# A two-layer MLP's second product: some operands built earlier, and the last ones in another order and on another engine

## The chip, the cores and the metric

The kernel runs on one NeuronCore of a Trainium2 chip. TensorE (PE) multiplies, VectorE (DVE), ScalarE (ACT) and GpSimd (POOL) do the elementwise work, and SyncE (SP) issues most DMAs. The metric is the device time of one execution in microseconds; a result is the median of the runs made.

## The reference, cut to what matters

The reference is a transformer block on 1024 tokens of width 1024: two attention branches, gates, an output projection, a squared-ReLU MLP and a last RMSNorm. The change touches its end alone:

```python
h2 = rms_norm(x, norm_mlp_g[l], NORM_EPS)
x = x + jnp.square(jax.nn.relu(h2 @ w_ff1[l])) @ w_ff2[l]      # 1024 -> 4096 -> 1024
return rms_norm(x, norm_final_g, NORM_EPS)
```

## The kernel before, in words

Everything is float32, but a matmul takes its operands in a shorter format. So each operand is split into two halves: `hi`, a copy by ScalarE in that format (line 1273), and `lo`, what is left, `x - hi`, by VectorE or GpSimd (line 1274). A product is then three matmuls: hi by hi, hi by lo and lo by hi (lines 1358 to 1360). `operand(x, to, eng)` makes the two halves, with `eng` for the lower one.

The second MLP product sums over 4096 hidden units, which are worked through in pairs of 128-blocks: 16 pairs of 256. The hidden activations `f` lie in DRAM, written by the first product (`squared`, line 1147), and are read back as raw blocks `ra`; the weights come as raw blocks `rb`. There are five groups: pairs 0 and 1 (the first group), pairs 2 to 5, 6 to 9 and 10 to 13, and at the end pairs 14 and 15.

A group is a 2 by 2 block product: the output is split into two halves of the tokens and two halves of the columns, the sum into two halves as well. Each of the first four groups uses seven block products instead of eight, in the order of `PRODUCTS`: 1, 5, 6, 3, 7, 2, 4. Product 1 multiplies raw blocks. Products 5, 6 and 3 take running sums: `fs5` of the activations (line 1302) and `ws5` of the weights (line 1310), which are overwritten from one product to the next. `a5` and `b5` are the halves of product 5's operands, and so on. In the first group a product is 24 matmuls, in the next three groups it is 48. Sums that two outputs share wait in `sum5` and `sum6`; the PSUM results are added into the residual (`xb` and `acc`, lines 1371 and 1373).

The last group, pairs 14 and 15, is done without the seven products: for each block of 128 tokens the four halves `alast` and `blast` are multiplied, column half 0 first, then column half 1 (`last_product`), and the final norm follows for that token block.

Where a raw block lies is fixed by a table of tiles (`HOME`) which the last pair of the first MLP product still reads, so its loads start as that product lets go of one tile after another. The halves of products 3, 6 and 4 of the first group lie partly in tiles (`own`) whose room was that of the first MLP product's results `c`: they can be written when the last `f` block has been written to DRAM. The residual `xb` is loaded into the same room, with the same wait.

The program's text does not set the order on an engine alone: a scheduler merges the instructions of neighbouring parts into one queue for each engine, and an engine takes its queue strictly in order. So an instruction that waits holds up all that stand behind it.

Of the kernel before, what the change touches and what calls it, by code (L numbers as in the profile page):

```python
# [77 lines left out]
def f(ap):  # L78

    return ap.bitcast(F32)  # L80
# [3 lines left out]
def tile_hybrid_block(ctx: ExitStack, tc: tile.TileContext, t: dict, out: bass.AP):  # L84
    nc = tc.nc
# [847 lines left out]
    for n in range(len(steps) + LAG):  # L933
        if n < len(steps):
            h, qb = steps[n]
# [10 lines left out]
        if 0 < n <= len(steps):  # L946
            h, qb = steps[n - 1]
            b_combine(heads[h], qb)
        later()
        if n >= LAG:  # L950
            h, qb = steps[n - LAG]
# [40 lines left out]
    for u in range(8 * AH + LAGA):  # L992
        h, n = u // 8, u % 8
# [108 lines left out]
    for n in range(16):  # L1102
# [9 lines left out]
        for j in range(4):  # L1112
            i = 4 * half + j
# [46 lines left out]
    def ff1_operands(n, ra, rb):  # L1160
        if n == NEARLY - 1:
            s1 = p5.tile([P, DK, P], F32, tag="u", name=f"s1_{n}", bufs=2)
        else:
            s1 = pf.tile([P, DK, P], F32, tag="s1", name=f"s1_{n}", bufs=2)
        return rest_operands(f"f{n}", ra, rb, s1)
# [18 lines left out]
    n = NEARLY - 1  # L1184
    operands = []
# [15 lines left out]
    for i, n in enumerate(order):  # L1201
        if i:
# [3 lines left out]
            operands = ff1_operands(n, *cur)  # L1206
# [11 lines left out]
    def place(nm, z, name, dt=F32):  # L1218
        pool = phb if nm in ("B11", "B21") else pht
        return pool.tile([P, GROUP, 512], dt, tag=f"h{nm}{z}", name=name)  # L1220
# [35 lines left out]
    def own(tag, name):  # L1256
        return p5.tile([P, GROUP, 512], F32R, tag=tag, name=name)

    def operand_set(name):

        sets[0] ^= 1
        if sets[0]:
            return {side: [place(nm, z, f"{side}{name}_{z}", F32R) for z in range(2)] for side, nm in (("a", "B11"), ("b", "B21"))}
        return {"a": [place("T3", 1, f"a{name}_0", F32R), own("a1", f"a{name}_1")],
                "b": [own("b0", f"b{name}_0"), own("b1", f"b{name}_1")]}

    def couple(to, c):
        return {side: [z[:, 2 * c:2 * c + 2, :] for z in to[side]] for side in "ab"}

    def operand(x, to, eng):  # L1270

        hi, lo = to
        nc.scalar.activation(hi, x, AF.Copy)  # L1273
        eng.tensor_tensor(lo, x, f(hi), op=ALU.subtract)  # L1274
        return hi, lo


    PRODUCTS = ((1, 0), (5, 0), (6, 1), (3, 1), (7, 0), (2, 0), (4, 1))

    def ff2_group(pairs, r, count):  # L1280
        begin = pairs[0] == 0
        couples = range(len(pairs) // 2)
        temp = {}

        def block(kind, i, j, c):
            return r.get((kind, i, j, c))

        def fresh(side, name, c):
            temp[side, c] = wp.tile([P, 2, 512], F32, tag="wh" if side == "a" else "wl", name=name, bufs=3)
            return temp[side, c]  # L1290

        def prepare(which, c, to):
            name = f"{which}_{pairs[2 * c]}"
            a = {1: (0, 0), 2: (0, 1), 4: (1, 1)}.get(which)
            b = {1: (0, 0), 2: (1, 0), 3: (1, 1)}.get(which)
            if a:
                s = block("a", *a, c)
            else:
                s = fresh("a", f"fs{name}", c) if which in (5, 7) else temp["a", c]
                x, y, op = {5: (block("a", 1, 0, c), block("a", 1, 1, c), ALU.add), 6: (s, block("a", 0, 0, c), ALU.subtract),  # L1300
                            3: (block("a", 0, 1, c), s, ALU.subtract), 7: (block("a", 0, 0, c), block("a", 1, 0, c), ALU.subtract)}[which]
                nc.vector.tensor_tensor(s, x, y, op=op)  # L1302
            if b:
                u = block("b", *b, c)
            else:

                u = temp["b", c] if which in (6, 4) else block("b", 1, 1, c) if which == 7 else fresh("b", f"ws{name}", c)
                x, y = {5: (block("b", 0, 1, c), block("b", 0, 0, c)), 6: (block("b", 1, 1, c), u),
                        4: (block("b", 1, 0, c), u), 7: (block("b", 1, 1, c), block("b", 0, 1, c))}[which]
                nc.vector.tensor_tensor(u, x, y, op=ALU.subtract)  # L1310
            return operand(s, to["a"], nc.vector), operand(
                u, to["b"], nc.vector if which == 1 or begin and which == 5 else nc.gpsimd)

        def target(which):
            if which in (5, 6):
                if begin:
                    sums[which] = place("T4", which - 5, f"sum{which}")
                return sums[which]
            half, col = {1: (0, 0), 2: (0, 0), 3: (0, 1), 4: (1, 0), 7: (1, 1)}[which]
            return res[half][:, :, 512 * col:512 * col + 512]  # L1320

        def begin_places(k, which):

            if k % 4 == 0 and k < 5:
                late["set"] = {side: [place(nm, z, f"{side}{which}_0_{z}", F32R) for z in range(2)]
                               for side, nm in (("a", "B11"), ("b", "B21"))}
            if k in (0, 1, 4, 5):
                return couple(late["set"], k % 4)
            if k == 2:
                x, y = place("T3", 1, "a6_0", F32R), place("T3", 0, "b6_0", F32R)  # L1330
            elif k == 3:
                x, y = own("a1", "a3_0"), own("b0", "b3_0")
            else:
                x, y = own("b1", "a4_0"), place("T3", 1, "b4_0", F32R)
            return {"a": [x[:, 0:2, :], x[:, 2:4, :]], "b": [y[:, 0:2, :], y[:, 2:4, :]]}

        banks = [None, None]
        for k, (which, more) in enumerate(PRODUCTS):
            if begin:
                ops = [prepare(which, 0, begin_places(k, which))]  # L1340
            else:
                to = operand_set(f"{which}_{pairs[0]}")
                ops = [prepare(which, c, couple(to, c)) for c in couples]
            if not more:
                if (k + count) % 2:
                    banks[k % 2] = [bank([P, 512], tag, f"p{which}_{pairs[0]}_{j}") for j, tag in enumerate(("T", "T", "mm", "gm"))]
                else:
                    banks[k % 2] = [bank2(f"p{which}_{pairs[0]}_{j}") for j in range(2)]
            here = banks[k % 2]
            target_of = target(which)  # L1350
            for j in range(4):
                wide = len(here) == 2
                acc = here[j // 2][:, 512 * (j % 2):512 * (j % 2) + 512] if wide else here[j]
                c = slice(j * P, j * P + P)
                for i in range(len(pairs)):
                    (ah, al), (bh, bl) = ops[i // 2]
                    last = i == len(pairs) - 1
                    nc.tensor.matmul(acc, ah[:, i % 2, c], bh[:, i % 2, :], start=i == 0 and not more, stop=False, skip_group_check=bool(more))  # L1358
                    nc.tensor.matmul(acc, ah[:, i % 2, c], bl[:, i % 2, :], start=False, stop=False, skip_group_check=bool(more))  # L1359
                    nc.tensor.matmul(acc, al[:, i % 2, c], bh[:, i % 2, :], start=False, stop=last, skip_group_check=bool(more))  # L1360
                if wide and j % 2 == 0:
                    continue
                into = target_of[:, j - 1:j + 1, :] if wide else target_of[:, j, :]
                of = here[j // 2].rearrange("p (j n) -> p j n", j=2) if wide else acc
                if begin and which in (5, 6):
                    nc.scalar.activation(into, of, AF.Copy)
                elif begin and which == 1:

                    x = wp.tile([P, 2, 512], F32, tag="wh", name=f"p1_0_{j}", bufs=3)
                    nc.scalar.activation(x, of, AF.Copy)  # L1370
                    nc.vector.tensor_tensor(into, x, into, op=ALU.add)
                else:
                    nc.vector.tensor_tensor(into, of, into, op=ALU.add)
            if begin and which == 6:
                load_b(pairs, r, 1, 0)
# [22 lines left out]

    r = pair_raws((NP2 - 2, NP2 - 1))
    blocks_a, blocks_b = {}, {}  # L1400
    for i in range(2):
        to = operand_set(f"last{i}")
        for j in range(2):
            blocks_a[i, j] = operand(r["a", i, j, 0], couple(to, j)["a"], nc.vector)
        for h in range(2):
            blocks_b[h, i] = operand(r["b", h, i, 0], couple(to, h)["b"], nc.gpsimd)
    for x in (res[0][:, :, 512:1024], res[1][:, :, 0:512], sums[5]):
        nc.vector.tensor_tensor(x, x, sums[6], op=ALU.add)
    nc.vector.tensor_tensor(res[1][:, :, 512:1024], res[1][:, :, 512:1024], sums[5], op=ALU.add)
# [17 lines left out]
    i = NT - 1  # L1427
    ss = p5.tile([P, 2], F32, tag="n_ss2", name="n3_last_ss")
    sq = wp.tile([P, D], F32, tag="wr", name="n3_last_sq", bufs=2)
    for h in range(2):  # L1430
# [3 lines left out]
        a = acc1[i][:, cols]  # L1434
# [35 lines left out]
```

## Time and profile before

| | us |
|---|---|
| median of 3 runs | 1673.32 |
| lowest, highest run | 1667.09, 1675.45 |
| profiled execution | 1674.86 |
| its span | 1673.1 |
| TensorE busy in the span | 1557.9 (93%) |
| VectorE busy | 1181.4 (71%) |
| ScalarE busy | 697.6 (42%) |
| GpSimd busy | 585.3 (35%) |

The second MLP product takes the stretch from 1333 us to the end. TensorE is busy nearly throughout. The share of VectorE, 71% over the span, is far higher there: 48.10 of the 50 us from 1350 to 1400, 49.86 of those from 1550 to 1600. An engine's mean share says little here; what counts is where TensorE stands still, and what it waits for.

### The profile page before, as it was taken

The page shows a single profiled execution, that of the slowest core. Times are in us where ns is not written, and L with a number is a line of the kernel's source. Part 1 is how long each engine was busy: PE and PEld are TensorE (multiplying, and loading weights), DVE is VectorE, ACT ScalarE, POOL GpSimd, SP SyncE. Part 2 cuts the span into 40 slices and gives each one's busy share as a digit, 9 for nine tenths or more (in the row PEclk, how much of TensorE's full clock was granted, in tenths as well). Part 3 has the DMA queues.
Part 4 walks back from the last instruction along what each step waited for, and adds up shares of the span by engine and source line. Part 5 has one row for each costly group of instructions (what it writes and reads, how often), then busy time and mean ns, then how long its engine had stood idle before and what let it go on. Part 6 is the DMA issues. An engine that isn't in the chain of part 4 may idle for free. (4 is left out here: it accounts for less than half of the span.)

```text
span 1673.1 us, 20932 instructions
## 1 busy us (share of the span) xinstructions
PE 1557.9 (93%) x7832; PEld 1299.2 (78%) x7832; DVE 1181.4 (71%) x1367; ACT 697.6 (42%) x1064; POOL 585.3 (35%) x289
## 2 busy tenths in 40 slices
PE   8899889988789998989999999899999989999998
PEld 6798667766577887988887878687888867888776
DVE  5976798698688996645547357644355599898984
ACT  4432122232467774544433236444444552333331
POOL 1534444555232332012220003533333344354551
PEclk8999899998999999999999999999999999999999
DMA  6367566555767557656557333444333571423112
GB/s 214 125 210 215 164 196 223 175 184 163 263 194 233 200 191 271 204 180 215 156 162 278 110 130 94 120 128 130 114 101 101 179 268 51 163 74 116 51 38 101
DMA packets 214389, 271.23 MB, mean 162 GB/s; under 512 B 12784, under 2 KB 136848, under 8 KB 214288
## 3 DMA queue, kind: packets, MB, share of 16 engines
q1 hardware_dynamic: 200464, 236.33, 44.4%
q10 hardware_dynamic: 13824, 33.56, 5.3%
q8 instruction: 62, 1.02, 0.3%
q14 instruction: 39, 0.32, 0.1%
HBM read 183.81 MB, written 80.27 MB: 158 GB/s over the span
## 5 line engine op out<-in xcount | busy, mean ns | idle before, releaser
L1359 PE MATMUL p<-b,a 128*128 128x512 f32 x392 | 154.7, 395 | 5.1 <-DVE b L1274 5.1
L1358 PE MATMUL p<-b,a 128*128 128x512 f32 x392 | 154.2, 393 | 3.0 <-ACT a L1273 3.0
L1360 PE MATMUL p<-b,a 128*128 128x512 f32 x392 | 154.4, 396 | 2.0 <-DVE a L1274 1.9
L1274 POOL TENSOR_TENSOR b<-ws,b 128x1024 fp32r<-128x1024 f32 x20 | 61.4, 3088 | 95.3 <-ACT b L1273 85.3
L1359 PEld LDWEIGHTS p<-b,a 128*128 128x128 f32 x392 | 74.2, 189 | 23.0 <-DVE b L1274 6.0
L1274 POOL TENSOR_TENSOR b<-rb,b 128x1024 fp32r<-128x1024 f32 x21 | 70.8, 3390 | 54.7 <-ACT b L1273 46.7
L1360 PEld LDWEIGHTS p<-b,a 128*128 128x128 f32 x392 | 74.0, 189 | 20.1 <-DVE a L1274 3.9
L1358 PEld LDWEIGHTS p<-b,a 128*128 128x128 f32 x392 | 74.1, 189 | 19.8 <-ACT a L1273 3.4
L689 PE MATMUL sb<-kb,qb 128*128 128x512 f32 x256 | 74.7, 416 | 15.1 <-ACT p L694 8.8
L694 ACT ACTIVATE p<-sb,mn 128x1024 f32<-128x1024 f32 x64 | 71.3, 1116 | 38.5 <-DVE mn L692 23.7
L692 DVE TENSOR_REDUCE mn<-sb 128x1 f32<-128x1024 f32 x64 | 76.8, 1217 | 9.7 <-PE sb L689 9.2
L265 DVE TENSOR_TENSOR s<-w 128x512 f32<-128x512 f32 x15 | 16.2, 1081 | 85.8 <-DMA w<-in_w_ff 85.8
L156 POOL TENSOR_SCALAR n_y<-n_ss 128x1 f32<-128x1 f32 x23 | 5.1, 222 | 187.7 <-ACT n_xn L163 183.2
L803 PE MATMUL sa<-kh_a,zq 128*128 128x256 f32 x256 | 68.9, 300 | 1.2 <-DVE mna L812 1.2
L828 DVE TENSOR_TENSOR pta<-ta,pta 128x512 fp32r<-128x512 f32 x64 | 43.8, 688 | 33.9 <-ACT pta L827 33.7
L689 PEld LDWEIGHTS sb<-kb,qb 128*128 128x128 f32 x256 | 45.9, 192 | 27.9 <-ACT p L694 13.1
L1273 ACT ACTIVATE a<-fs 128x1024 fp32r<-128x1024 f32 x28 | 29.4, 1054 | 90.6 <-PE p L1359 71.3
L803 PE MATMUL sa<-kl_a,zq 128*128 128x256 f32 x256 | 65.8, 288 | 0.0
L246 POOL TENSOR_TENSOR wt_f_l<-w,wt_f_h 128x1024 fp32r<-128x1024 f32 x15 | 36.1, 2404 | 83.0 <-ACT wt_f_h L245 70.2
L816 ACT ACTIVATE sm<-sm,mna 128x512 f32<-128x512 f32 x64 | 46.1, 720 | 32.4 <-DVE mna L812 31.8
L827 ACT ACTIVATE pta<-ta 128x512 fp32r<-128x512 f32 x64 | 37.6, 591 | 52.2 <-PE ta L823 44.5
L1145 ACT ACTIVATE c<-c 128x512 f32<-128x512 f32 x64 | 39.9, 624 | 46.6 <-DVE c L292 34.9
(442 smaller groups left out, 4966.4 us busy)
## 6 DMA issues: line engine op xcount, KB each, us to landing
w<-in_w_in SPq DMA_DIRECT2D x32, 512.0 KB, 4.3
qk<-r ACTq DMA_DIRECT2D x32, 512.0 KB, 4.8
f<-c ACTq DMA_DIRECT2D x64, 256.0 KB, 2.0
rb<-in_w_ff SPq DMA_DIRECT2D x32, 512.0 KB, 4.6
ra<-f SPq DMA_DIRECT2D x64, 256.0 KB, 5.0
w<-in_w_ff SPq DMA_DIRECT2D x30, 512.0 KB, 4.2
vb<-vb SPq DMA_DIRECT2D x16, 512.0 KB, 6.6
rot<-raw SPq DMA_DIRECT2D x64, 128.0 KB, 4.5
```

Source lines behind the costliest of these rows:

```text
L689: nc.tensor.matmul(sps[:, 512 * n:512 * n + 512], q[:, z, (qb % 4) * P:(qb % 4 + 1) * P], o.k[m][:, 512 * n:512 * n + 512], start=z == 0, ...
L692: nc.vector.tensor_reduce(mn, sps, axis=AX.X, op=ALU.min)
L694: nc.scalar.activation(p, sps, AF.Exp, scale=-1.0, bias=mn, accum_out=o.zz[qb][:, m:m + 1])
L803: nc.tensor.matmul(ps[:, 0:CM], zq[:, n % 4, c, :], kk[:, c * CM:(c + 1) * CM], start=c == 0 and kk is o.kh, stop=c == NCLS - 1 and kk is ...
L816: nc.scalar.activation(sm, sm, AF.Exp, scale=-1.0, bias=mn, accum_out=stat[h % 2][:, n:n + 1])
L827: nc.scalar.activation(view[0], tv, AF.Copy)
L828: nc.vector.tensor_tensor(view[1], tv, f(view[0]), op=ALU.subtract)
L1145: nc.scalar.activation(c, c, AF.Relu)
L1274: eng.tensor_tensor(lo, x, f(hi), op=ALU.subtract)
L1358: nc.tensor.matmul(acc, ah[:, i % 2, c], bh[:, i % 2, :], start=i == 0 and not more, stop=False, skip_group_check=bool(more))
L1359: nc.tensor.matmul(acc, ah[:, i % 2, c], bl[:, i % 2, :], start=False, stop=False, skip_group_check=bool(more))
L1360: nc.tensor.matmul(acc, al[:, i % 2, c], bh[:, i % 2, :], start=False, stop=last, skip_group_check=bool(more))
```

## The change

Two places. In the first group, `prepare` was called for each product just ahead of its matmuls; now, at product 1, the operands of products 1 and 5 are both prepared ahead of product 1's matmuls, and the others at their products as before. In the last group, the halves were written in the order of the first index of two loops: the activations of token half 0, the weights of column half 0, then those of half 1, with every lower half of a weight on GpSimd. Now the weights of column half 0 come first, then the activations of token half 0, the weights of column half 1, the activations of token half 1; and the lower halves of the two weight blocks of column half 1 are VectorE's. What is computed, and where it is stored, is the same.

```diff
@@ -1335,9 +1335,13 @@
         banks = [None, None]
+        ready = {}
         for k, (which, more) in enumerate(PRODUCTS):
             if begin:
-                ops = [prepare(which, 0, begin_places(k, which))]
+
+                for n in (0, 1) if k == 0 else (k,) if k > 1 else ():
+                    ready[n] = [prepare(PRODUCTS[n][0], 0, begin_places(n, PRODUCTS[n][0]))]
+                ops = ready.pop(k)
             else:
@@ -1398,12 +1402,13 @@
     r = pair_raws((NP2 - 2, NP2 - 1))
     blocks_a, blocks_b = {}, {}
-    for i in range(2):
-        to = operand_set(f"last{i}")
+    to = [couple(operands, z) for operands in (operand_set("last0"), operand_set("last1")) for z in range(2)]
+    for side, i in (("b", 0), ("a", 0), ("b", 1), ("a", 1)):
         for j in range(2):
-            blocks_a[i, j] = operand(r["a", i, j, 0], couple(to, j)["a"], nc.vector)
-        for h in range(2):
-            blocks_b[h, i] = operand(r["b", h, i, 0], couple(to, h)["b"], nc.gpsimd)
+            if side == "a":
+                blocks_a[i, j] = operand(r["a", i, j, 0], to[2 * i + j]["a"], nc.vector)
+            else:
+                blocks_b[j, i] = operand(r["b", j, i, 0], to[2 * i + j]["b"], nc.vector if i else nc.gpsimd)
```

What the scheduler makes of it shows in the engines' queues. In the rows below a name's middle number is the first pair of its group, the last number a serial one.

VectorE at the passage from the first MLP product (`c..._15`) to product 1 and product 5 of the first group, before:

```order
L1274 TENSOR_TENSOR a1_0_1_11477<-ra00_0_11450,a1_0_0_11476 128x1024
L292 TENSOR_TENSOR c12_15_11367<-zf15_11371,c12_15_11367 128x512
L294 TENSOR_TENSOR c21_15_11368<-zf15_11371,u_15_11366 128x512
L1310 TENSOR_TENSOR ws5_0_11518<-rb11_0_11461,ws5_0_11518 128x1024
L295 TENSOR_TENSOR c22_15_11369<-zf15_11371,c21_15_11368 128x512
L298 TENSOR_TENSOR c21_15_11368<-4f15_11372,c21_15_11368 128x512
L1302 TENSOR_TENSOR fs5_0_11516<-ra10_0_11455,ra11_0_11458 128x1024
L1274 TENSOR_TENSOR a1_0_1_11477<-fs5_0_11516,a1_0_0_11476 128x1024
```

And now:

```order
L1274 TENSOR_TENSOR a1_0_1_11477<-ra00_0_11450,a1_0_0_11476 128x1024
L1302 TENSOR_TENSOR fs5_0_11484<-ra10_0_11455,ra11_0_11458 128x1024
L292 TENSOR_TENSOR c12_15_11367<-zf15_11371,c12_15_11367 128x512
L294 TENSOR_TENSOR c21_15_11368<-zf15_11371,u_15_11366 128x512
L1274 TENSOR_TENSOR a1_0_1_11477<-fs5_0_11484,a1_0_0_11476 128x1024
L295 TENSOR_TENSOR c22_15_11369<-zf15_11371,c21_15_11368 128x512
L1302 TENSOR_TENSOR fs5_0_11484<-fs5_0_11484,ra00_0_11450 128x1024
L298 TENSOR_TENSOR c21_15_11368<-4f15_11372,c21_15_11368 128x512
L1310 TENSOR_TENSOR ws5_0_11486<-rb11_0_11461,ws5_0_11486 128x1024
```

The activation operand of product 5 (`fs5` and the lower half made of it, which shares a tile with product 1's and so is printed as `a1`) moved ahead of the last four additions of the first MLP product, and the next sum `fs5` of product 6 moved ahead of the weight sum.

ScalarE from the last copies of the first MLP product on, before (`sum5` and `p1` are copies out of PSUM):

```order
L1147 DMA f15_9039<-c21_15_11368 128x512
L1370 ACTIVATE p1_0_1_11498<-p1_0_0_11484 128x1024
L1370 ACTIVATE p1_0_3_11513<-p1_0_1_11485 128x1024
L1273 ACTIVATE b3_0_11595<-rb11_0_11461 128x1024
L1273 ACTIVATE a1_0_0_11476<-fs5_0_11516 128x1024
L1273 ACTIVATE a4_0_11704<-ra11_0_11458 128x1024
L1366 ACTIVATE sum5_11528<-p5_0_0_11524 128x512
L1366 ACTIVATE sum5_11528<-p5_0_1_11525 128x512
L1273 ACTIVATE a6_0_11557<-fs5_0_11516 128x1024
```

And now:

```order
L1374 ACTIVATE p1_0_1_11506<-p1_0_0_11492 128x1024
L1146 ACTIVATE c21_15_11368<-c21_15_11368 128x512
L1374 ACTIVATE p1_0_3_11521<-p1_0_1_11493 128x1024
L1147 DMA f15_9039<-c21_15_11368 128x512
L1370 ACTIVATE sum5_11528<-p5_0_0_11524 128x512
L1370 ACTIVATE sum5_11528<-p5_0_1_11525 128x512
L1273 ACTIVATE b6_0_11558<-ws5_0_11486 128x1024
L1370 ACTIVATE sum5_11528<-p5_0_2_11526 128x512
L1273 ACTIVATE a3_0_11594<-fs5_0_11484 128x1024
L1370 ACTIVATE sum5_11528<-p5_0_3_11527 128x512
L1273 ACTIVATE b3_0_11595<-rb11_0_11461 128x1024
```

The upper half of product 5 is out of this piece (it stands earlier); that of `b6`, which stood ahead of the first row shown of before, now stands behind two copies of product 5's results, and `a3`, which product 3's lower half on VectorE waits for, behind three.

VectorE at the last group, the difference (`sum6` is the last shared sum, `ff_last0` the first token block's result):

```order
-L1408 TENSOR_TENSOR acc1_8065<-acc1_8065,sum6_11565 128x4x512
-L1274 TENSOR_TENSOR alast1_1_13297<-ra10_14_13271,alast1_0_13296 128x1024
-L1274 TENSOR_TENSOR alast1_1_13297<-ra11_14_13274,alast1_0_13296 128x1024
-L1423 TENSOR_TENSOR xb_11471<-ff_last0_13312,xb_11471 128x1024
...
+L1413 TENSOR_TENSOR acc1_8065<-acc1_8065,sum6_11565 128x4x512
+L1274 TENSOR_TENSOR blast1_1_13291<-rb01_14_13269,blast1_0_13290 128x1024
+L1274 TENSOR_TENSOR blast1_1_13291<-rb11_14_13277,blast1_0_13290 128x1024
+L1274 TENSOR_TENSOR alast1_1_13289<-ra10_14_13271,alast1_0_13288 128x1024
+L1274 TENSOR_TENSOR alast1_1_13289<-ra11_14_13274,alast1_0_13288 128x1024
+L1428 TENSOR_TENSOR xb_11471<-ff_last0_13312,xb_11471 128x1024
```

The two lower halves of the weights of column half 1 stand on VectorE ahead of those of the activations of token half 1; GpSimd's queue has lost two instructions there. TensorE's queue now begins the second token block while it waits for the first of them.

## Rows read from the trace of the kernel before

**Rows 1.** Waits of TensorE, 1300 to 1420 us: total us, times, longest

```profile
PE p L1359 <- DVE b L1274: 5.1, 2, 5.0
PE p L1358 <- ACT a L1273: 3.0, 1, 3.0
PE p L1360 <- DVE a L1274: 1.3, 2, 0.9
```

**Rows 2.** Waits of TensorE, 1590 us to the end

```profile
PE ff_last L1416 <- POOL blast L1274: 3.0, 2, 1.6
```

**Rows 3.** Timeline, TensorE: start us, us, what, [idle before <- releaser]

```profile
1333.18 0.39 PE L1358 MATMUL p<-b,a 128*128 128x512 f32 x1
...
1338.42 0.39 PE L1360 MATMUL p<-b,a 128*128 128x512 f32 x1
1341.81 0.50 PE L1358 MATMUL p<-b,a 128*128 128x512 f32 x1 [3.00 <-ACT a L1273]
...
1360.45 0.40 PE L1359 MATMUL p<-b,a 128*128 128x512 f32 x1
...
1376.74 0.39 PE L1358 MATMUL p<-b,a 128*128 128x512 f32 x1
...
1383.90 0.79 PE L1359 MATMUL p<-b,a 128*128 128x512 f32 x1 [4.96 <-DVE b L1274]
```

**Rows 4.** Stretch of product 1, second group: length; busy us (instructions) by engine; clock, DMA

```profile
1376.74:1395.20 18.46, 13.35 (x49) 10.21 (x48) 16.67 (x14) 2.01 (x2) 5.78 (x2) 0.82 0.19 58
```

**Rows 5.** Timeline, VectorE, first group

```profile
1335.20 3.40 DVE L1302 TENSOR_TENSOR fs<-ra,ra 128x1024 f32<-128x1024 f32 x1
1341.79 2.56 DVE L1274 TENSOR_TENSOR a<-fs,a 128x1024 fp32r<-128x1024 f32 x1 [3.19 <-ACT a L1273]
1344.28 1.21 DVE L1310 TENSOR_TENSOR rb<-rb,rb 128x1024 f32<-128x1024 f32 x1
...
1371.36 0.68 DVE L1373 TENSOR_TENSOR xb<-p,xb 128x512 f32<-128x512 f32 x1
...
1380.49 3.35 DVE L1274 TENSOR_TENSOR b<-rb,b 128x1024 fp32r<-128x1024 f32 x1
```

**Rows 6.** Timeline, GpSimd, first group

```profile
1335.12 2.40 POOL L1274 TENSOR_TENSOR b<-ws,b 128x1024 fp32r<-128x1024 f32 x1 [11.99 <-ACT b L1273]
...
1351.23 9.03 POOL L1274 TENSOR_TENSOR b<-rb,b 128x1024 fp32r<-128x1024 f32 x1 [7.95 <-DVE xb L1371]
...
1376.98 5.78 POOL L1274 TENSOR_TENSOR b<-ws,b 128x1024 fp32r<-128x1024 f32 x2 [10.03 <-PE p L1360]
```

**Rows 7.** Timeline, ScalarE and its DMA queue, first group

```profile
1336.63 0.85 ACTq L1147 DMA_DIRECT2D f<-c  x2
...
1340.71 1.05 ACT L1273 ACTIVATE a<-fs 128x1024 fp32r<-128x1024 f32 x1
```

**Rows 8.** Timeline, SyncE's queue, first group

```profile
1322.72 4.23 SPq L1229 DMA_DIRECT2D ra<-f  x6
...
1339.49 1.74 SPq L1389 DMA_DIRECT2D xb<-x  x4
```

**Rows 9.** DMA issues, 1315 to 1420 us: count, KB each, median us to landing

```profile
ra<-f SPq DMA_DIRECT2D x30, 256.0 KB, 5.5
...
xb<-x SPq DMA_DIRECT2D x4, 512.0 KB, 6.4
```

**Rows 10.** Timeline, last group: TensorE, ScalarE, VectorE, GpSimd

```profile
1617.60 0.39 PE L1415 MATMUL ff_last<-blast,alast 128*128 128x512 f32 x1
...
1626.39 0.50 PE L1416 MATMUL ff_last<-blast,alast 128*128 128x512 f32 x1 [1.64 <-POOL blast L1274]
...
1617.56 2.01 ACT L1273 ACTIVATE alast<-ra 128x1024 fp32r<-128x1024 f32 x2 [7.00 <-PE p L1359]
...
1620.73 6.68 DVE L1274 TENSOR_TENSOR alast<-ra,alast 128x1024 fp32r<-128x1024 f32 x2
...
1620.59 5.74 POOL L1274 TENSOR_TENSOR blast<-rb,blast 128x1024 fp32r<-128x1024 f32 x2 [5.05 <-ACT blast L1273]
```

## The prediction

> **What bounds the kernel now.** I read the waits of TensorE first, then the timelines round the long ones. TensorE is busy 93% of the span, so time can only be won where it stands still. In the second MLP product it does so in two places: in the first group and at the passage to the second, 5.1 + 3.0 + 1.3 = 9.4 us [rows 1]; and at the last group, 3.0 us in two waits for GpSimd's lower halves [rows 2]. Elsewhere, from 1395 to 1617 us, it is fed. At full clock 23 matmuls take 1338.42 - 1333.18 = 5.24 us, 0.228 each [rows 3]; a product of the first group takes 5.47 us.
>
> The three waits of the first group have two causes. At product 5 TensorE waits 3.00 us for the upper half of `a5`, which ScalarE copies at 1340.71 [rows 3, 7], then 1.3 in two waits for lower halves [rows 1]. At 1383.90 it has waited 4.96 us for the lower half of the second weight block of the second group, which VectorE ends at 1380.49 + 3.35 = 1383.84 [rows 3, 5]: VectorE has worked without a break since 1341.79 and is simply late. [...]
>
> VectorE and GpSimd get in each other's way. An instruction of VectorE on 128x1024 that is alone takes 1.21 and starts the next after 1.13 (the overlap is 0.07); `fs5` at 1335.20 took 3.40, because GpSimd's at 1335.12 ran until 1337.52 [rows 5, 6]. Seven instructions were stretched so between 1335.2 and 1383.8, the first and the last in [rows 5]; their excess adds up to 10.9 us.
>
> **The change, part A: the first group.** I walked the four queues of the new order through with the durations of before, in the clock of the old trace; all of these times are estimates.
> - `fs5` can start when `ra11` has landed: the six issues end at 1322.72 + 4.23 = 1326.95, landing takes 5.5 [rows 8, 9], so about 1332.0 instead of 1335.2. Product 5's upper half is then ready at 1334.2, the lower one at 1335.5. The waits of product 5 and those behind it (3.0 + 1.3 = 4.3 us [rows 1]) go.
> - Two additions of the first MLP product are now behind it, and they free the PSUM bank of product 1's second half: at 1336.1, TensorE wants it at 1335.9. Cost 0.3, between 0 and 0.7.
> - What is late next is product 6. Its weight sum is ready at 1339, but ScalarE copies the upper half only after the last `c` results, two copies of product 1 and two of product 5's results, with three DMA issues of about 0.43 each [rows 7] among them: 1343.4 to 1344.45. GpSimd's lower half is there 2.4 later [rows 6], at 1346.9; TensorE wants it at 1344.65. Cost 2.3, between 1.2 (copies closer together) and 5 (GpSimd shut out).
> - VectorE meanwhile stands before the lower half of `a3`, whose upper half ScalarE makes at 1345.0 at the earliest, behind three copies of product 5's results. It is idle from about 1341.2 to 1346 and nothing behind it can pass: 4.8 us, where 3.19 were lost before [rows 5]. The loads of `xb`, which wait for the last `f` write, are issued near 1344.3 instead of 1339.49 [rows 8] and land 6.4 later [rows 9], just as VectorE comes to them: 0.5.
> - Product 7 starts at 1358 (its second matmul at 1358.5 against 1360.45 [rows 3]), product 1 of the second group at 1374.9 against 1376.74. TensorE has won 4.3 - 0.3 - 2.3 = 1.7 us, some 1.9 with the restarts.
> - Then the late block again. From `fs5` to the second weight block of the second group VectorE has 38 instructions, 26 on 128x1024 at 1.13 and 12 on 128x512 at 0.68 - 0.07 [rows 5]: 36.7 us. (Four small additions came in, two sums of 1.13 each went behind it.) With 5.3 idle and collisions with seven GpSimd instructions, which I placed one by one at 8.2 (10.9 before; bounds 4 and 11), it ends at 1332.0 + 50.2 = 1382.2 instead of 1383.84, 1.6 earlier. And TensorE's queue now has 14 instead of 7 matmuls ahead of that wait: 7 x 0.228 = 1.6. Gain at this point 1.6 + 1.6 = 3.2 us (TensorE's lead of 1.9 is contained in it); TensorE still waits about 4 us there, and I let the slow clock after it stay as it is. From there to 1617 I expect nothing: TensorE is fed and keeps its lead.
>
> **Part B: the last group.** TensorE starts it at 1617.60 and after the second wait reaches its 24th matmul at 1626.39 [rows 10]; without waits that is 1617.60 + 23 x 0.228 = 1622.8. So 3.0 us of waits [rows 2] and 0.5 of restarts can go. Now ScalarE's upper halves of the two blocks are there by 1618.5 + 2 = 1620.5 (it starts at 1617.56 and one activation copy is ahead [rows 10]). VectorE's sum ends at 1620.73, where its next instruction starts [rows 10], so the lower halves are done at 1621.9 and 1623.05. TensorE, which now runs seven matmuls of the second token block in between, wants them at 1622.2 and 1623.6. Both in time; GpSimd has nothing left then, so the pair of `alast` lower halves, 6.68 us against GpSimd's 5.74 [rows 10], shrinks to 2.3 as well, and the first addition to `xb`, which frees a PSUM bank, is not later. Gain 3.5; bounds 2.0 (the lower halves late by 0.7 twice) and 3.6.
>
> [...]
>
> **Sum.** 3.2 + 3.5 = 6.7 us off the profiled execution's 1674.86 (span 1673.1 and 1.8 around it). That execution is 1.5 above the median 1673.3, so the median goes to 1666.6.
>
> **Rivals.**
> 1. VectorE is not late at the second group. If the collisions cost 4 instead of 8.2 and `a3` is reached without a stop, the late block is ready at 1377.5, before TensorE's 14 matmuls from 1374.9 are through at 1378.1. Then the wait and the slow clock go: 1.8 + 5.1 + 2.4 = 9.3, with part B 12.8 us, 1660.5. For it: GpSimd's work falls partly into VectorE's new gap. Against it: VectorE's queue is longer in that stretch, not shorter.
> 2. Part A gives nothing back, the tail alone counts. Place: GpSimd's lower half for product 7, wanted at 1358.2. If it is passed over again, 9.03 from 1355.1, it is there at 1364.1, product 7 starts 3.7 later than before, and the second group's late block is then held up by product 4 alone; it costs less by as much. Near 3.5 in all: 1669.8. Against it: two instructions behind its issue VectorE comes to additions out of PSUM, and these let GpSimd in.
> 3. Slower. Place: the lower half of `a3` at the head of VectorE's queue. Its tile was the `c` results' room, so it waits for the last `f` write as well as for ScalarE. Each us that this comes later than 1346 moves VectorE's whole queue by one, up to the second group's block, and `xb` with it. It eats part A after 3.2 us and the tail after 6.7: from a stop of 11.5 us on the kernel is slower. With a stop of 14, 1676. The `f` write took about 2 us after its issue in the trace (issued by 1337.48, `xb` released at 1339.49 [rows 7, 8]), which speaks against it.
>
> **How the numbers follow.** Forecast 0.48 (its own range 1663.5 to 1669.0), rival 1 0.24 (1657 to 1663), rival 2 0.20 (1668 to 1672), rival 3 0.08 (1674 to 1684). Cutting about a tenth at each end, the range is 1658.5 to 1672.5. Half a per cent is 8.4 us, about what a measurement of this kernel can tell from no change: its own three runs are that far apart. Faster than 1664.9: all of rival 1 and a fifth of the forecast, 0.35. Slower than 1681.7: a third of rival 3 and a little, 0.04. The rest 0.61.
>
> **What would show it.** Right, if TensorE no longer waits for `a5` at product 5; waits 1 to 3 us at product 6 for GpSimd; VectorE has one gap of 4 to 5 us before `a3`; TensorE's wait at product 1 of the second group is still there, 3 to 5 us, with a slow clock after it; and no wait for lower halves is left in the last group. Wrong, if the second group's wait is gone (then 1660), if product 7 waits for GpSimd over 4 us, or if the last group still waits, for VectorE instead.

## The result, and the profile after

Twelve runs of each kernel on the same chip: 1662.2 us (1656.45 to 1664.3) against 1667.74 (1665.31 to 1675.57), a ratio of 0.9945 with a 95% interval of 0.9929 to 0.9961. By the ratio that is 9 us, 6.5 to 11.8; by the medians 5.5. The forecast was 6.7 off, a ratio of 0.996. Its absolute number, 1666.6, stands 4.4 above the median, because the three runs that it started from (1673.32) lay above the twelve of this series. So 1662.2 lies in the stated range, but among the times that the prediction gave to its rival 1 (1657 to 1663), below the forecast's own 1663.5 to 1669.0. The time alone does not choose between the two; the traces do.

The profiled spans, 1673.1 and 1661.7, differ by 11.4 us. That is too much: 3.46 of it was there before product 1's first matmul (1333.18 before, 1329.72 after), in a part of the program that is the same in both. Among all the kernels of this document this start lies anywhere from 1323 to 1333 us. So I compare two stretches inside the second MLP product: **A**, from product 1's start in the first group to the last group's start, and **B**, from there to the end. Between matmuls, A went from 284.42 to 280.04 and B from 55.50 to 51.94: 4.4 + 3.6 = 7.9 us, inside the measured interval.

TensorE's waits after, 1300 to 1420 us (answers to [rows 1]; total us, times, longest):

```profile
PE p L1363 <- DVE b L1274: 3.8, 1, 3.8
PE p L1363 <- POOL b L1274: 2.3, 2, 1.2
```

From 1590 us to the end there is none, where [rows 2] had 3.0. The lines moved by four: L1362 to L1364 are the matmuls, L1374 and L1370 ScalarE's copies, L1375 and L1377 the additions. The timeline of TensorE round the waits, against [rows 3]:

```profile
1329.72 0.39 PE L1362 MATMUL p<-b,a 128*128 128x512 f32 x1
...
1342.16 0.50 PE L1363 MATMUL p<-b,a 128*128 128x512 f32 x1 [1.14 <-POOL b L1274]
...
1354.51 0.50 PE L1363 MATMUL p<-b,a 128*128 128x512 f32 x1 [1.18 <-POOL b L1274]
...
1378.06 0.80 PE L1363 MATMUL p<-b,a 128*128 128x512 f32 x1 [3.79 <-DVE b L1274]
...
1609.76 0.39 PE L1420 MATMUL ff_last<-blast,alast 128*128 128x512 f32 x1
```

Product 5 waits for nothing any more; product 6 and product 7 wait a little for GpSimd; the wait for the late block at the second group has stayed, 3.79 instead of 4.96. Product 1 of the second group, against [rows 4] (length, busy us by engine, clock, DMA):

```profile
1370.92:1387.29 16.37, 12.59 (x50) 10.01 (x49) 15.32 (x13) 2.12 (x3) 5.70 (x2) 0.90 0.25 84
```

2.1 us shorter. In both traces the clock is slow behind the wait: before, nine matmuls took 4.00 us (1383.90 to 1387.90) instead of 9 x 0.228 = 2.05, which cost 1.9; after, seven took 3.08 (1378.06 to 1381.14) instead of 1.60, which cost 1.5. The granted clock of the 4 us behind the wait reads 0.50 before and 0.63 after:

```profile
1383.90:1387.90 4.00, 4.00 (x9) 3.13 (x10) 3.67 (x4) 0.00 (x0) 0.00 (x0) 0.50 0.43 135
```

```profile
1378.06:1382.06 4.00, 4.00 (x12) 3.24 (x13) 2.95 (x4) 1.06 (x1) 0.00 (x0) 0.63 0.44 132
```

So 0.5 of the 2.1 is the clock, 1.3 is waiting (5.1 against 3.8), and the rest, 0.3, I put down to the restarts behind the waits (at a clock of 1.00 the first matmul behind a wait reads 0.50 us, the others 0.39). VectorE, GpSimd, ScalarE and SyncE, against [rows 5 to 8]:

```profile
1327.87 1.22 DVE L1302 TENSOR_TENSOR fs<-ra,ra 128x1024 f32<-128x1024 f32 x1
...
1341.17 2.02 DVE L1274 TENSOR_TENSOR a<-fs,a 128x1024 fp32r<-128x1024 f32 x1 [3.87 <-ACT a L1273]
...
1371.35 3.37 DVE L1274 TENSOR_TENSOR a<-ra,a 128x1024 fp32r<-128x1024 f32 x1
...
1375.78 2.23 DVE L1274 TENSOR_TENSOR b<-rb,b 128x1024 fp32r<-128x1024 f32 x1
```

```profile
1339.72 2.38 POOL L1274 TENSOR_TENSOR b<-ws,b 128x1024 fp32r<-128x1024 f32 x1 [20.07 <-ACT b L1273]
...
1351.12 6.69 POOL L1274 TENSOR_TENSOR b<-rb,b 128x1024 fp32r<-128x1024 f32 x2 [5.66 <-ACT b L1273]
```

```profile
1338.60 1.05 ACT L1273 ACTIVATE b<-ws 128x1024 fp32r<-128x1024 f32 x1
...
1340.02 1.06 ACT L1273 ACTIVATE a<-fs 128x1024 fp32r<-128x1024 f32 x1
```

```profile
1338.48 1.74 SPq L1393 DMA_DIRECT2D xb<-x  x4
```

`fs5` now starts 1.9 us ahead of product 1's first matmul, where it started 2.0 behind it. VectorE then stands for 3.87 us before `a3`'s lower half and ends the late block at 1375.78 + 2.23 = 1378.01. In the last group, against [rows 10], VectorE's queue alone tells the story; all four lower halves take 1.2 each, since GpSimd has nothing left:

```profile
1612.90 2.35 DVE L1274 TENSOR_TENSOR blast<-rb,blast 128x1024 fp32r<-128x1024 f32 x2
1615.17 2.35 DVE L1274 TENSOR_TENSOR alast<-ra,alast 128x1024 fp32r<-128x1024 f32 x2
```

### The profile page after: what moved, and what is told of

Read it like the earlier page. It is cut to its first block, busy times and chain, and to the rows that moved or that the text cites. A ratio compares the mean times of both kernels' runs of the same rounds, so it can differ in the third digit from the quotient of the medians.

```text
span 1661.7 us, 20931 instructions
## 1 busy us (share of the span) xinstructions
PE 1557.9 (94%) x7832; PEld 1300.6 (78%) x7832; DVE 1181.4 (71%) x1369; ACT 699.0 (42%) x1064; POOL 577.9 (35%) x287
## 4 chain that ended last, share of the span: by engine, by line
PE 35%; DVE 7%; issue 3%; DMA 2%; POOL 2%; ACT 1%; SPq 0%; DVEq 0%; POOLq 0%; ACTq 0%
PE yf L237 5%; PE zf L237 5%; PE p L1364 3%; PE p L1363 3%; PE p L1362 3%; PE 4f L237 2%; DVE a L1274 2%; PE f0f L237 2%; PE f1f L237 2%; PE wo L1116 2%; PE wo L1118 2%; PE wo L1117 2%; DMA rb<-in_w_ff 1%; DVE fs L1302 1%; PE ya L1063 1%
## 5 line engine op out<-in xcount | busy, mean ns | idle before, releaser
L1364 PE MATMUL p<-b,a 128*128 128x512 f32 x392 | 154.9, 395 | 0.7 <-DVE a L1274 0.7
L1362 PE MATMUL p<-b,a 128*128 128x512 f32 x392 | 153.5, 392 | 0.0
L1364 PEld LDWEIGHTS p<-b,a 128*128 128x128 f32 x392 | 74.0, 189 | 17.9 <-DVE a L1274 1.8
L1362 PEld LDWEIGHTS p<-b,a 128*128 128x128 f32 x392 | 73.9, 188 | 16.4
L1274 POOL TENSOR_TENSOR b<-rb,b 128x1024 fp32r<-128x1024 f32 x21 | 65.6, 3141 | 46.8 <-ACT b L1273 46.2
```

## The experiments

Here A and B are taken between the first weight loads of the lines, 0.2 us ahead of the matmuls (so B reads 0.2 more). Each comes from the one profiled execution of its kernel, with the ends read to 0.1 us, so a difference can be off by 0.1. Kernels that are alike in a stretch show how far these numbers scatter: A 279.7 to 280.2 in four of them, 284.4 and 284.8 in two. Ratios are to the kernel before.

| kernel | A | B | ratio, 95% interval |
|---|---|---|---|
| before | 284.4 | 55.7 | |
| after | 280.0 | 52.2 | 0.9945, 0.9929 to 0.9961 |
| first_only | 279.7 | 55.7 | 0.9979, 0.9962 to 0.9997 |
| last_only | 284.8 | 52.1 | 0.9984, 0.9966 to 1.0002 |
| last_order | 279.7 | 56.6 | 0.9987, 0.9968 to 1.0005 |
| last_engine | 280.2 | 52.2 | 0.9954, 0.9932 to 0.9975 |
| three_ahead | 278.2 | 52.2 | 0.9942, 0.9920 to 0.9964 |
| late_block_pool | 278.4 | 52.2 | 0.9937, 0.9914 to 0.9960 |
| a4_pool | 281.1 | 52.1 | 0.9947, 0.9929 to 0.9966 |
| four_ahead | 280.5 | 52.2 | 0.9954, 0.9935 to 0.9972 |
| four_late | 278.4 | 52.2 | 0.9936, 0.9913 to 0.9959 |
| three_late | 278.4 | 52.2 | 0.9931, 0.9906 to 0.9956 |
| before_late | 283.4 | 55.6 | 0.9981, 0.9962 to 1.0001 |
| vector_relief | 276.6 | 52.2 | one run |

**Each place alone.** first_only is the change without its second hunk, last_only without its first.

> The changed kernel with the last group as it was before; only the first group's early operands are left of the change. Measures: A is the time from product 1's first matmul in the first group to the last group's first matmul (284.42 us in the profile before, 280.04 after), B the time from there to the end of the span (55.50 before, 51.94 after). Theory of two separate gains: A 280.0 (279.5 to 280.5), B 55.5, and 4.4 us off the kernel before, a ratio of 0.9974. Rival (the first group's lead is swallowed before the end, only the tail counts): A 284, ratio 0.999 to 1.001.

> The kernel before with the changed last group alone. Theory of two separate gains: A 284.4, B 51.9, both waits for GpSimd's lower halves gone, 3.6 us off, a ratio of 0.9979; this and the first group's 4.4 us add up to the whole change. Rival (the last group only gains because the first group's change lets VectorE arrive earlier): B 54 to 55.5, ratio 0.999 to 1.000.

Both as the first theory had it: A falls by 4.7 and B stays; B falls by 3.6 and A stays. The gains are separate, and 4.7 + 3.6 = 8.3 is the whole change's 7.9 within the scatter. In the times alone the first is just told from nothing, and the second is not: its interval reaches 1.0002.

**The last group: order or engine?** last_order:

```diff
-blocks_b[j, i] = operand(r["b", j, i, 0], to[2 * i + j]["b"], nc.vector if i else nc.gpsimd)
+blocks_b[j, i] = operand(r["b", j, i, 0], to[2 * i + j]["b"], nc.gpsimd)
```

last_engine, the old loops:

```diff
-blocks_b[h, i] = operand(r["b", h, i, 0], couple(to, h)["b"], nc.gpsimd)
+blocks_b[h, i] = operand(r["b", h, i, 0], couple(to, h)["b"], nc.vector if i else nc.gpsimd)
```

> The changed kernel, with the new order in the last group, but all lower halves of weights on GpSimd again. Theory that both parts are needed: GpSimd takes 2.4 to 2.9 us for each lower half, starts them 2 us after the group's first matmul and VectorE's sums lie beside it; TensorE, which now comes to the first one straight after 13 matmuls, waits 2.0 to 3.5 us in two waits; B 53.9 to 55.4 against 51.94. Rival that the order alone does it (GpSimd starts a microsecond earlier, so the wait is gone): B 52 to 52.5.

> The changed kernel, with the old order in the last group, but the lower halves of column half 1 on VectorE. Theory that both parts are needed: VectorE makes the activations' lower halves first, so those of the weights end about 6.5 and 7.7 us after the group's first matmul where TensorE wants them at 4.6 and 6.0 us: one wait of 1.9 us for VectorE, B 53.8. Rival that the engine alone does it (VectorE is so much faster than GpSimd that its order does not matter): B 52 to 52.5.

The order alone does harm: 56.6 is 0.9 above before, and above the 53.9 to 55.4 that I had expected; the two waits sum to 3.9 instead of 2.0 to 3.5. TensorE and GpSimd in last_order:

```profile
1614.53 0.50 PE L1421 MATMUL ff_last<-blast,alast 128*128 128x512 f32 x1 [2.27 <-POOL blast L1274]
...
1617.83 0.50 PE L1421 MATMUL ff_last<-blast,alast 128*128 128x512 f32 x1 [1.64 <-POOL blast L1274]
```

```profile
1611.12 6.66 POOL L1274 TENSOR_TENSOR blast<-rb,blast 128x1024 fp32r<-128x1024 f32 x2 [4.25 <-ACT blast L1273]
```

GpSimd starts 2 us into the group, as expected, but takes 3.3 for each half beside VectorE's (two for 6.66 there too), and TensorE comes to the first after 13 matmuls.

The engine alone does everything, against my expectation. VectorE in last_engine, whose last group starts at 1607.89:

```profile
1611.03 2.35 DVE L1274 TENSOR_TENSOR alast<-ra,alast 128x1024 fp32r<-128x1024 f32 x2
1613.30 2.35 DVE L1274 TENSOR_TENSOR blast<-rb,blast 128x1024 fp32r<-128x1024 f32 x2
```

The halves end 6.5 and 7.7 us into the group, exactly as I had written, and nobody waits. What I had wrong was when TensorE wants them: I took that from the changed kernel's queue. In this kernel the scheduler merges 30 matmuls, 30 x 0.228 = 6.8 us, ahead of the first, where it has 20 in the changed kernel, 17 before and 13 with the order alone.

**The late block.** Each of the next four is one edit of the changed kernel. three_ahead (four_ahead has 0 to 3):

```diff
-for n in (0, 1) if k == 0 else (k,) if k > 1 else ():
+for n in (0, 1, 2) if k == 0 else (k,) if k > 2 else ():
```

> The changed kernel, with the operands of product 6 prepared ahead of product 1's matmuls too, so that ScalarE copies the upper half of b6 before the copies of product 1's results instead of behind two of product 5's. Measures: A from product 1's first matmul to the last group's (280.0 us in the changed kernel), B from there to the end (52.2). Theory 1 (ScalarE's order is what product 6 waits for, and the time is set by VectorE's late block at the passage to the second group): the wait of 1.14 at product 6 goes, A stays at 280.0 within 0.7, because VectorE's queue is not moved, and TensorE waits as much longer, near 5, for the late block. Theory 2 (each wait of TensorE costs its own length): A falls to 278.8 or less.

A fell by 1.8, the second theory's number, but not by its mechanism. The wait at product 6 is gone, yet product 7 now waits 1.80, and 11 matmuls run in the 4 us behind it, where 18 do at a clock of 1.00 (behind product 7's wait in the changed kernel; the rows are in the last section). What paid is VectorE, which I had said would not move: two of its lower halves, the first two of these rows, now miss GpSimd's instructions and take 1.2 instead of 2.02 and 3.37.

```profile
1340.88 1.23 DVE L1274 TENSOR_TENSOR a<-fs,a 128x1024 fp32r<-128x1024 f32 x1 [3.78 <-ACT a L1273]
...
1370.51 1.22 DVE L1274 TENSOR_TENSOR a<-ra,a 128x1024 fp32r<-128x1024 f32 x1
...
1372.87 2.47 DVE L1274 TENSOR_TENSOR b<-rb,b 128x1024 fp32r<-128x1024 f32 x1
```

The late block, the third row, ends 2.5 us earlier after product 1's start, and TensorE's wait for it is 0.5.

late_block_pool:

```diff
-u, to["b"], nc.vector if which == 1 or begin and which == 5 else nc.gpsimd)
+u, to["b"], nc.vector if which == 1 and (begin or c == 0 or pairs[0] > 2) or begin and which == 5 else nc.gpsimd)
```

> The changed kernel, with the lower half of the second weight block of product 1, second group, on GpSimd instead of VectorE, which is the late block. Theory 1 (VectorE being late sets the passage): GpSimd is idle from 1361.2 to 1371.2 in the changed kernel's trace and the upper half is there at 1369.4, so the lower half ends near 1372.6 where TensorE, with 7 matmuls ahead of it, wants it at 1372.5; the wait of 3.8 goes, and the 1.4 us of slow clock behind it: A 274.8 to 276. Theory 2 (GpSimd is kept out by VectorE as in the 9.03 us of before): it ends at 1378.4, the wait is 5.9, A 281 to 282. Rival: the wait is only passed on to the next halves (product 5 of the second group, GpSimd's pair behind it): A 278 to 279.

The first theory was right about the late block: GpSimd took 3.06, and of the wait and the slow clock there 0.58 is left, for a half of the activations. The gain is 1.6 instead of 4 to 5, because TensorE now runs into VectorE three products later. The number, 278.4, is the one that the expectation gave to its rival, and the wait was indeed passed on, but not to where the rival had it (product 5, GpSimd's pair). The waits at product 3 of the second group, absent in the changed kernel:

```profile
1405.68 0.50 PE L1364 MATMUL p<-b,a 128*128 128x512 f32 x1 [1.30 <-DVE a L1274]
...
1408.67 0.50 PE L1364 MATMUL p<-b,a 128*128 128x512 f32 x1 [1.34 <-DVE a L1274]
```

a4_pool:

```diff
-return operand(s, to["a"], nc.vector), operand(
+return operand(s, to["a"], nc.gpsimd if begin and which == 4 else nc.vector), operand(
```

> The changed kernel, with the lower half of product 4's activations in the first group on GpSimd instead of VectorE; GpSimd has it ahead of the two halves that product 7 waits for. Theory 1 (VectorE's late block sets the time, TensorE's shorter waits ahead of it are covered by it): product 7 waits for GpSimd 2 to 4.5 us instead of 1.18, VectorE reaches the late block 1.1 to 2.8 us earlier, A 277 to 279 all the same. Theory 2 (each wait of TensorE costs its own length): A 281 to 283.

A grew to 281.1, the second theory's number. TensorE's wait at product 7 was not covered. VectorE lost what it had won: its sum beside GpSimd's new instruction was stretched, and then it stood for results that TensorE, waiting and slow, gave late.

```profile
1344.63 3.42 DVE L1310 TENSOR_TENSOR rb<-rb,rb 128x1024 f32<-128x1024 f32 x1
...
1356.71 1.23 DVE L1377 TENSOR_TENSOR acc<-p,acc 128x1024 f32<-128x1024 f32 x1 [2.50 <-PE p L1364]
```

four_ahead:

> The changed kernel, with the operands of products 6 and 3 prepared ahead of product 1's matmuls too. ScalarE then copies the upper half of a3, for which VectorE stands idle for 3.87 us, behind two copies of product 5's results instead of three, near 1339.0 instead of 1340.02, but no earlier than the last write of the hidden activations lets go of its tile (1338.2). Theory 1 (VectorE's queue sets the time): VectorE's gap shrinks by 0.5 to 1.5 us, the late block is earlier by as much, A 278.5 to 279.5, and B 52.2. Theory 2 (GpSimd is the one that decides by product 7): A stays at 280 or grows, with product 7's wait above 2.

VectorE's gap shrank to 3.11 and the late block came 1.3 earlier, as expected. But A is 280.5, only 0.3 above the highest of the four kernels that are alike. That is the second theory's number without its mechanism: product 7 did not wait, and product 4 just 0.4 for GpSimd. At the second group TensorE, let through sooner, waited 1.0 and 3.4 for VectorE, and the slow clock lasted longer than in the changed kernel:

```profile
1374.40:1378.40 4.00, 4.00 (x11) 3.09 (x10) 2.23 (x4) 1.06 (x1) 0.00 (x0) 0.50 0.42 135
1378.40:1382.40 4.00, 4.00 (x17) 3.29 (x16) 3.53 (x5) 0.00 (x0) 0.00 (x0) 0.88 0.00 0
```

**Combined, and from the other side.** The same edits together (four_late, three_late), and the late block's edit on the kernel before (before_late); the three expectations stand in this order.

> Four products' operands ahead and the late block's lower half on GpSimd, both together, on the changed kernel. With the late block on GpSimd alone A was 278.4 instead of 280.0: the wait of 3.8 and the slow clock behind it went, but two waits of 1.3 for VectorE's lower halves came at product 3 of the second group, which were not there before. Theory (VectorE is the bound of this stretch, and TensorE, once let through, runs into it a group later): four ahead brings VectorE's queue forward by 1.3 us and takes 1.9 us of waits at products 6 and 7 away, so A is 276.0 to 277.5, with waits of 1 to 3 us for VectorE left in the second group. Rival (what four ahead costs, 280.5, is due to the order of ScalarE, and the late block was not its cause): A 278.5 to 279.5.

> Three products' operands ahead and the late block's lower half on GpSimd, on the changed kernel. Three ahead alone gave A 278.2, with a wait of 1.8 at product 7 for GpSimd and 11 instead of 17 matmuls in the 4 us behind it, and VectorE reached the late block 2.5 us earlier than in the changed kernel. Theory (VectorE is the bound): the late block's wait was already down to 0.5 there, so taking it away gives 0.5 at most there and 1.2 more from the three waits for VectorE later on, since VectorE has an instruction and a collision less: A 276.5 to 278. Rival (the two edits are independent and add up, 1.8 + 1.6): A 276.6 and below.

> The kernel before, with the lower half of the late block (second weight block of product 1, second group) on GpSimd, and nothing else. Theory (VectorE's place sets where the first group ends): VectorE's late block ended 50.8 us after product 1's first matmul before and 48.5 in the changed kernel; the wait of 5.0 and 2.4 us of slow clock go, VectorE is run into later as in the changed kernel, so A is that kernel's 278.4 + 2.3 = 280.7 (280 to 281.5), 3.7 less than before. Rival (the waits at product 5 stay and add up with all others): A 277.0, 284.4 - 7.4. Rival 2 (GpSimd is kept out by VectorE and hands the wait on): A 283 to 285.

Neither combination adds anything: both give 278.4, as late_block_pool alone did, outside what either theory had expected (276.0 to 277.5 and 276.5 to 278). The two waits of 1.3 at product 3 of the second group are in all three, whatever happened in the first group. In three_late VectorE is busy 39.97 of the 40 us up to them:

```profile
1364.00:1404.00 40.00, 37.34 (x161) 29.64 (x160) 39.97 (x28) 11.45 (x11) 21.51 (x7) 1.00 0.11 39
```

before_late missed: 283.4, the number of its second rival with the reverse mechanism. GpSimd was not kept out, VectorE was: the first weight block's lower half, still its own, took 3.36 beside GpSimd's, and TensorE waited 4.88 for that one instead.

```profile
1367.07 3.01 DVE L1274 TENSOR_TENSOR a<-ra,a 128x1024 fp32r<-128x1024 f32 x1
1370.00 3.36 DVE L1274 TENSOR_TENSOR b<-rb,b 128x1024 fp32r<-128x1024 f32 x1
```

**Less work for VectorE.** vector_relief is three_late with four additions left out:

```diff
-else:
+elif pairs[0] != 2 or which != 1:
     nc.vector.tensor_tensor(into, of, into, op=ALU.add)
```

> Three products ahead and the late block on GpSimd, as the run before it (A 278.4, with two waits of 1.3 for VectorE's lower halves at product 3 of the second group), and besides four additions of 128x512 on VectorE left out: those of product 1's results to the residual in the second group, so that part of the sum is not computed. They stand between product 5's and product 6's operands, 0.60 us each, 2.4 in all; ScalarE, GpSimd and TensorE keep their order. Theory (VectorE, busy without a break from the first group to there, sets the 278.4 that three different kernels had in common): the first wait goes, the second shrinks to 0.3 or goes with it, A 275.8 to 276.4. Rival (product 3 waits for ScalarE's upper half, which itself waits until TensorE lets go of the operand set): both waits stay, A 278.0 to 278.6.

A is 276.6, 1.8 less; one of the two waits went, the other is still 1.30. That is 0.2 above the theory's range and well below the rival's, by which ScalarE and TensorE's own release would have kept both waits. Where TensorE still waits, the whole 2.4 us came through: the matmul behind the wait of 1.34 in three_late starts 1403.78 - 1323.52 = 80.3 us after product 1's first one, the same matmul here 1405.34 - 1327.46 = 77.9. The 0.5 that A lacks was lost behind it; 0.3 of that are further waits for VectorE (0.9 instead of 0.6 us between 1430 and 1590 us).

```profile
1403.78 0.50 PE L1364 MATMUL p<-b,a 128*128 128x512 f32 x1 [1.34 <-DVE a L1274]
```

```profile
1405.34 0.51 PE L1364 MATMUL p<-b,a 128*128 128x512 f32 x1 [1.30 <-DVE a L1274]
```

So VectorE's work sets A there. One more thing differs between the two traces, which the edit does not explain: behind product 7's wait, 1.80 us in both, TensorE's clock fell in three_late (0.57 over the next 4 us, 1.7 us lost) and stayed full here (rows in the last section). TensorE so came to the second group 1.7 us sooner, which is why a wait of 1.30 was left. It does not account for the gain: with the slow clock TensorE would by this estimate have found its waits for VectorE here, 0.58 and 1.30, nearly used up, and A the same within some tenths.

No version is clearly better than the changed kernel. three_late has the lowest ratio, and its interval overlaps; by A it is 1.6 us ahead, 0.1%.

## Why the prediction was right, step by step

To compare clock readings, 3.46 us are added to those of after.

- **Product 5.** `fs5` was put at 1332.0 (the two terms given for it add up to 1332.45); it started at 1331.3, without a gap behind the instruction ahead of it, so it did not stand waiting for its load. The waits of 4.3 us are gone. Right. The PSUM bank (0.3) cost nothing.
- **Product 6.** Forecast 2.3, bounds 1.2 to 5; it was 1.14, just below the lower one. ScalarE's copies stand closer than I had them: `b6` at 1342.1, not 1343.4.
- **VectorE's stop at `a3`.** Forecast 4.8, until 1346; it was 3.87, until 1344.6, by the same copies. `xb` was issued at 1341.9 instead of 1344.3, and VectorE did not wait for it.
- **Product 7.** Forecast 0.5, for `xb`; it was 1.18, for GpSimd. That is the place of rival 2, but GpSimd's pair took 6.69, 3.35 each, not 9.03.
- **Collisions.** 8.2 forecast in seven instructions; seven, together 9.2 (each one's us less 1.21).
- **The late block.** Ready at 1382.2 by the forecast, at 1381.5 in the trace; wait about 4, in fact 3.79; 14 matmuls ahead of it, as the queue said. From product 1's first matmul it came 2.4 us earlier (50.66 to 48.29), where the forecast had 1.6. That VectorE took 50.1 us from `fs5` to its end, against 50.2 in the forecast, is luck in part: 1.4 less standing still and 1.0 more in collisions nearly cancel, and the work itself was 37.1, not 36.7.
- **The slow clock.** I put it at 2.4 and let it stay; rival 1 and the expectation of before_late use the same 2.4. It was an estimate: what 48 matmuls at 0.228 and 5.1 of waiting leave of product 1's stretch in [rows 4]. No run shows 2.4 of slow clock: counted from the end of the wait, the slow matmuls of before cost 1.9 us, and the rest of it I put down to restarts behind the waits. After, they cost 1.5. This term of 0.5 was missing.
- **Sum of part A.** 2.4 + 1.6 + 0.5 = 4.5, less 0.1 for TensorE's waits between 1420 and 1590 us (0.7 where there were 0.6), is the 4.4 of the trace. The forecast was 3.2: it had the late block's gain 0.8 too small and the clock's at nothing.
- **Part B.** 3.5 forecast, 3.56 measured, with ScalarE's copies there 2.9 us and VectorE's sum done 3.1 us into the group, both as worked out. But my reading that order and engine work together was not put to a test there, and fell in the experiments: the engine does it, and the order is not needed.

The rivals: VectorE was still late (against rival 1), the first group gave 4.4 back (against rival 2), and the stop at `a3` was 3.87 us, far from 11.5 (against rival 3). The prediction gave 0.61 to a change of less than half a per cent either way; the measured gain, 0.39 to 0.71%, lies on both sides of that line.

The 6.69 of GpSimd's pair for product 7 are 0.95 over 2.4 for each half, less than one VectorE instruction of 1.2. The 9.03 us of [rows 6] came again in before_late, in the same place, and are 6.6 over 2.4, the time of five. VectorE's first addition out of PSUM there stands in the second of these rows of before_late:

```profile
1342.64 9.03 POOL L1274 TENSOR_TENSOR b<-rb,b 128x1024 fp32r<-128x1024 f32 x1 [7.95 <-DVE xb L1371]
```

```profile
1349.32 1.88 DVE L1373 TENSOR_TENSOR xb<-p,xb 128x512 f32<-128x512 f32 x3
```

GpSimd ends at 1351.67, 2.35 us behind that addition's start, about its time alone (2.40 [rows 6]). In the kernel before it is the same: it ends at 1360.26, and the additions start at 1357.90, in the first of these rows; they took 1.88 there, and three others 1.87 while GpSimd stood idle, in the second:

```profile
1357.90 1.88 DVE L1373 TENSOR_TENSOR xb<-p,xb 128x512 f32<-128x512 f32 x3
...
1373.09 1.87 DVE L1373 TENSOR_TENSOR xb<-p,xb 128x512 f32<-128x512 f32 x3
```

So these rows fit what the prediction held against its rival 2, that GpSimd got its turn at the additions out of PSUM; why it did, no run shows. Elsewhere it came in between two subtractions of VectorE (the late block of [rows 5], 3.35 instead of 1.21); what decides that stays open.

What the prediction did not see is the bound behind its bound. Its rival 1 had the wait and the slow clock there worth their full length, once the late block is in time. Four kernels that had it earlier or on GpSimd stopped at A 278.2 to 278.4 (four_ahead and before_late did not get that far), and only leaving out work of VectorE's went below that.

## What to carry to other kernels

Where a busy engine feeds the one that you are speeding up, look at when its next operands come before you price a wait that you remove: here 5.3 us of wait and slow clock paid 1.6. Compare two marks inside the program rather than spans, when the rest of the program scatters by more than the change. And take the time at which an engine wants an operand from the queue of the kernel that you will run, not from its sister's: here the scheduler put 30 matmuls in front of the operand in the one and 20 in the other.

## What was not expected of the hardware

In these traces the length of a wait does not tell whether TensorE's clock falls behind it. Full clock was kept after 3.00 us (product 5 before, [rows 3]; the 4 us behind it read 1.00), after 1.14 and 1.18 (after: 18 matmuls in the 4 us behind each, 1.00), and after 2.27 and 1.64 (last_order: the matmuls behind them start 0.23 apart). It fell with 4.96 (before: 0.50) and 3.79 (after: 0.63), with 2.87 (a4_pool: 0.57 from 1353.50 to 1357.50, just behind it), and with 1.80 in three_ahead, where the granted clock of the 4 us that follow reads 0.61:

```profile
1349.50:1353.50 4.00, 2.24 (x10) 1.50 (x8) 4.00 (x6) 1.54 (x2) 3.33 (x2) 1.00 1.00 342
1353.50:1357.50 4.00, 3.97 (x11) 3.16 (x12) 4.00 (x3) 1.06 (x1) 4.00 (x2) 0.61 1.02 388
```

The program alone does not decide it either. three_late and vector_relief come to the same wait of 1.80 by the same instructions; three_late reads 0.57 in the 4 us behind it (and 0.80, with 15 matmuls, from 1349.50 to 1353.50), vector_relief, whose wait ends at 1351.48, kept full clock:

```profile
1349.50:1353.50 4.00, 2.20 (x10) 1.67 (x10) 4.00 (x6) 0.95 (x1) 4.00 (x2) 1.00 1.00 373
1353.50:1357.50 4.00, 4.00 (x19) 3.32 (x18) 4.00 (x3) 0.11 (x1) 4.00 (x2) 1.00 0.70 250
```

What tells these cases apart stays open; it also means that 1.6 us in a stretch of a single trace can be the clock alone, unless a later wait takes them up, as in vector_relief. At 0.61, 4 x 0.39 = 1.6 us are lost, nearly as much as the wait itself.

The other is the size of the loss when VectorE and GpSimd subtract at once: on 128x1024 VectorE took 1.2 alone and up to 3.4 beside GpSimd, which took 2.4 alone and mostly 2.8 to 3.4, in one place 9.0, beside VectorE. So here an instruction moved from the one to the other could cost more than it freed, as in a4_pool (A 1.1 longer), or leave most of the wait in place, as in before_late (4.88 of 4.96).
